# Products of ones at three places of the first block, and one doubling step by upper and lower rows

## The chip, the cores and the metric

The kernel runs on one core of one Trainium2 chip. The metric is device time in microseconds (us), the median over the runs of one launch of the whole program. The engines are TensorE (PE in the profile; its weight loads are PEld), VectorE (DVE), ScalarE (ACT), GpSimd (POOL) and SyncE (SP); here SP issues the DMA transfers.

## What is computed

A two-block network on 256 tokens of width 1024. The first block has two layers: layer 0 mixes tokens with two recurrences side by side (HGRN2 on one half of the width, RWKV7 on the other), layer 1 with attention. The second block has attention, pooling and a mixture of experts. All of the change lies in layer 0's mixer:

```python
def hgrn_rwkv_mixer(h, w_in, w_out, ...):
    u = h @ w_in
    hq, hf, hi, hg, ur = jnp.split(u, ...)
    f = lb + (1.0 - lb) * sigmoid(hf)
    o_a = hgrn2_chunked(silu(hq), 1.0 - f, hi, log(f))
    ...
    y = rwkv7_scan(r, decay, k, v, kk, a)
    o_b = (head_layer_norm(y) + bonus) * g
    return concatenate([o_a, o_b]) @ w_out

def rwkv7_scan(...):
    def step(state, inp):
        sa = einsum('bhvk,bhk->bhv', state, -kk_t)
        state = state * w_t + sa[..., None] * (kk_t * a_t) + v_t[..., None] * k_t
        return state, einsum('bhvk,bhk->bhv', state, r_t)
```

## The kernel before

**Projections.** Weights arrive in fp32 by DMA and are split into a high and a low part (`split_tile`, L112: a cast on ACT at L116, a subtraction on DVE at L117). A product in fp32 accuracy is then three products, high by high, low by high and high by low (`mm3`, L137 to L139). A group of 24 products of 256 columns makes 128 output columns; `dense_tok` makes the values `hv` with 48 products of 512 columns.

**RWKV7 by blocks.** The 256 tokens are two blocks of 128 (b = 0, 1), with 8 heads each, 16 in all. `El` (L556) holds the 128 by 128 lower triangles of all 16. The recurrence is solved by inverting unit lower triangles: the four diagonal blocks of 32 of each triangle go through DRAM (`dd`) into a layout in which DVE eliminates one column after another (`inverse`, L650 and L652: 31 steps of two operations). The result goes back through DRAM (L655, eight reads at L660), and four copies (`Ql`, L661) and four transposes (`Tu`, L664) put it on the diagonals.

**Doublings.** `levels` then joins blocks of 32 into blocks of 64 and those into 128. `first` multiplies `El` by `Tu` (L684), ACT copies the result to `Wm`, and `then` multiplies by `Ql` (L698 for 32, L708 for 64). At l = 32 each of the 8 triangles of a block has one product on its upper 64 rows and one on its lower 64 rows, taken in turn. After that `chain` (from L735) carries the state over the two blocks.

**HGRN2.** Beside this, the projections of `hE` (L800), of the queries `hq` (L816; four groups of 24 products) and of `hv` run, and then nine levels of a score matrix `ST`: DVE prepares `z` (L842, L843, L858, L859), TensorE multiplies it by itself (L865), DVE copies under a mask (L866; L833 for the diagonal).

**Order.** `fills` holds generators whose steps `tick` interleaves with the projections: `pairs` (the other triangles of RWKV7, L607 to L642) and `inverse` in turn, then `levels`, then `chain`. Within that, a scheduler sets each engine's final order; an engine issues in that order. Accumulators in PSUM come from pools: `psa` gives `acc` tiles from one pool of four, in the order of the program's text; `psb` gives `pb` tiles, `psf` gives `pf` tiles. A tile is given again once all uses of it four tiles earlier are done.

**Products of ones.** `spin(n)` (L361) takes one `acc` tile and puts n products of a constant `ones` into it that nobody reads. It stands at three places at the very start of the program.

Of the kernel before, what the change touches and what calls it, by code (L numbers as in the profile page):

```python
# [52 lines left out]
def tile_body(ctx, tc, a, out, stop=None, dbg=None):  # L53
    nc = tc.nc
    V, A, G, T = nc.vector, nc.scalar, nc.gpsimd, nc.tensor
# [12 lines left out]
    def psa():  # L68
        return pa.tile([128, 512], F32, name="acc")
# [17 lines left out]
    ones = const.tile([128, 1], F32, name="ones")  # L87
# [247 lines left out]
    def mixer0():  # L335
# [22 lines left out]
        G.iota(prow, pattern=[[0, 1]], base=0, channel_multiplier=1, allow_small_or_imprecise_dtypes=True)  # L358
        V.tensor_scalar(ident, trow, prow, None, op0=ALU.is_equal)

        def spin(n):  # L361
            p = psa()
            for i in range(n):
                T.matmul(p[:, 0:128], ones.to_broadcast([128, 128]), ones.to_broadcast([128, 128]), start=True, stop=True)
        spin(8)

        raw = [psb(), psb(), psb(), psf()]
# [10 lines left out]
        p = psa()  # L378
# [72 lines left out]
        for s, dst in ((0, ld), (1, ta)):  # L451
            for j2 in range(2):
                p = psb()
                for i in range(2):
                    j = 2 * j2 + i
# [8 lines left out]
        for j2 in range(2):  # L464
            sq = t2([128, 2, S], "sq")
            p = psb()
            for i in range(2):
                j = 2 * j2 + i
# [5 lines left out]
            for i in range(2):  # L474
                j = 2 * j2 + i
# [75 lines left out]
        for b in range(2):  # L551
            bs = slice(b * 128, b * 128 + 128)
            ps = psb(), psb()
            for j in range(4):
                for h in range(2):
                    T.matmul(ps[h][:, j * 128:(j + 1) * 128], al[hp[h], j, bs], bt[0][hp[h], j, bs], start=True, stop=True)  # L556
            for h in range(2):
                V.tensor_tensor(El[:, 8 * b:8 * b + 8, :].rearrange("p (j h) c -> p h j c", h=2)[:, h],
                                ps[h].rearrange("p (j c) -> p j c", j=4), m4(maskL, 4), mult)
# [20 lines left out]
        for b in range(2):  # L580
            p = psb()
# [15 lines left out]
        def pairs():  # L597
            for b in range(2):
                bs = slice(b * 128, b * 128 + 128)
                px = psa()  # L600
                ps = psb(), psb()
                for j in range(4):
                    for h in range(2):
                        T.matmul(ps[h][:, j * 128:(j + 1) * 128], bt[0][hp[h], j, bs], rh[hp[h], j, bs], start=True, stop=True)
                heads = lambda t: t.rearrange("p (j h) c -> p h j c", h=2)
                for h in range(2):
                    V.tensor_tensor(heads(Ebr[b])[:, h], ps[h].rearrange("p (j c) -> p j c", j=4), m4(maskR, 4), mult)  # L607
                yield
                for j2 in range(2):
                    ps = psb(), (psf, psb)[j2]()  # L610
                    for i in range(2):
                        for q_, r in enumerate((al, rh)):
                            for h in range(2):
                                T.matmul(ps[h][:, q_ * 256 + i * 128:q_ * 256 + i * 128 + 128], bt[1][hp[h], 2 * j2 + i, bs],
                                         r[hp[h], 2 * j2 + i, bs], start=True, stop=True)
                    eka = RW.tile([128, 2, 2, 128], F32, name="eka")
                    for h in range(2):
                        V.tensor_tensor(eka[:, h], ps[h][:, 0:256].rearrange("p (i c) -> p i c", i=2), m4(maskA, 2), mult)
                    yield
                    for h in range(2):  # L620
                        V.tensor_tensor(heads(Ekr[b])[:, h, 2 * j2:2 * j2 + 2], ps[h][:, 256:512].rearrange("p (i c) -> p i c", i=2),
                                        m4(maskR, 2), mult)
                    for i in range(2):
                        for h in range(2):
                            hs = slice((2 * j2 + i) * 128 + h * 64, (2 * j2 + i) * 128 + h * 64 + 64)
                            T.matmul(px[:, hs], eka[:, h, i, :], vt[:, b, hs], start=True, stop=True)
                    yield
                A.copy(X[b], px)

            for j2 in range(2):  # L630
                p, p2 = psb(), psf()
                for i in range(2):
                    j = 2 * j2 + i
                    T.matmul(p[:, i * 256:(i + 1) * 256], rk64[:, j, :], rx[:, j, :], start=True, stop=True)
                    T.matmul(p2[:, i * 256:(i + 1) * 256], g2w[:, j * 128:(j + 1) * 128], gd, start=True, stop=True)
                js = slice(2 * j2, 2 * j2 + 2)
                V.tensor_tensor(bon[:, js, :], p.rearrange("p (i t) -> p i t", i=2), vx[:, js, :], mult)
                for i in range(2):
                    j = 2 * j2 + i
                    g = p2[:, i * 256:(i + 1) * 256]  # L640
                    A.activation(gt[:, j, :], g, AF.Copy, scale=col("ln_w", j))
                    V.scalar_tensor_tensor(bon[:, j, :], bon[:, j, :], col("ln_b", j), g, op0=add, op1=mult)  # L642
                yield
# [22 lines left out]
        def mixed(a_, b_):  # L666

            live = [a_, b_]
            while live:
# [2 lines left out]
                        live.remove(g)  # L672
                yield

        def levels():


            def first(l, b):
                o = 8 * b
                Wm = t2([128, 8, l], "Wm")  # L680
                p = psb()[:, 0:8 * l]
                for i in range(8):
                    for r in ((0, 64) if l == 32 else (64,)):
                        T.matmul(p[(r if l == 32 else 0):(r + 64 if l == 32 else 64), i * l:i * l + l],  # L684
                                 El[r:r + 64, o + i, (r if l == 32 else 0):(r + 64 if l == 32 else 64)],
                                 Tu[r:r + 64, o + i, (r + 32 if l == 32 else 64):r + 64], start=True, stop=True)
                n = 128 if l == 32 else 64
                A.copy(Wm[0:n], p[0:n].rearrange("p (h c) -> p h c", h=8))
                return l, b, Wm
# [136 lines left out]
        for l in range(9):  # L826
# [33 lines left out]
            if m < 128:  # L860
                for b in range(2):
                    bs = slice(b * 128, b * 128 + 128)
                    p = psa()
                    for h in range(4):
                        T.matmul(p[:, h * 128:(h + 1) * 128], z[:, h, bs], z[:, h, bs], start=True, stop=True)  # L865
                    V.copy_predicated(part(ST[:, b], l - 1, 1), half4(lvl[:, l - 1, :], l - 1, 1, 4),  # L866
                                      part(p.rearrange("p (h c) -> p h c", h=4), l - 1, 1))
                tick()
                if l == 4:
                    tick(100)  # L870
                    fills.append(chain())
                    tick(2)
            else:
                p = psa()
                for h in range(4):
                    T.matmul(p[:, h * 128:(h + 1) * 128], z[:, h, 0:128], z[:, h, 128:256], start=True, stop=True)
                A.copy(STx, p.rearrange("p (h c) -> p h c", h=4))
# [1157 lines left out]
```

## Time and profile before

| what | value |
|---|---|
| median of 3 runs | 1330.45 us (1330.16 to 1331.88) |
| profiled execution | 1331.68 us, of which its span 1329.8 us |
| PE busy | 1164.5 us, 88% |
| DVE busy | 717.6 us, 54% |
| ACT busy | 497.6 us, 37% |
| mean granted TensorE clock | 0.935 of full |

The span is the time between the first and the last instruction of the trace; 1.9 us of the profiled execution lie around it. The chain that ended last is PE for 52%, DMA for 27% and DVE for 11% of the span. From about 890 us on the expert weights stream at 420 GB/s without a gap; before that TensorE is busy for nine tenths or more of nearly every slice, with the granted clock below full in some.

### The profile page before, as it was taken

The page shows a single profiled execution, that of the slowest core. Times are in us where ns is not written, and L with a number is a line of the kernel's source. Part 1 is how long each engine was busy: PE and PEld are TensorE (multiplying, and loading weights), DVE is VectorE, ACT ScalarE, POOL GpSimd, SP SyncE. Part 2 cuts the span into 40 slices and gives each one's busy share as a digit, 9 for nine tenths or more (in the row PEclk, how much of TensorE's full clock was granted, in tenths as well). Part 3 has the DMA queues.
Part 4 walks back from the last instruction along what each step waited for, and adds up shares of the span by engine and source line. Part 5 has one row for each costly group of instructions (what it writes and reads, how often), then busy time and mean ns, then how long its engine had stood idle before and what let it go on. Part 6 is the DMA issues. An engine that isn't in the chain of part 4 may idle for free.

```text
span 1329.8 us, 18843 instructions
## 1 busy us (share of the span) xinstructions
PE 1164.5 (88%) x7392; PEld 849.3 (64%) x7392; DVE 717.6 (54%) x1293; ACT 497.6 (37%) x870; POOL 208.1 (16%) x218
## 2 busy tenths in 40 slices
PE   8899789999999999999999999898877676777765
PEld 7888787988988888898999888662322121212222
DVE  4768866676777887657665689861112010101112
ACT  7626325454444656546444555620000000000002
POOL 4500010222221351122222232300000000000000
PEclk9899799999999999999999999999987896967797
DMA  8342116768785553667775853699999999999996
GB/s 276 116 119 96 17 65 218 263 240 286 281 291 187 176 184 127 220 232 245 259 246 174 335 190 147 233 366 414 420 422 421 421 420 420 422 418 423 419 422 269
DMA packets 129503, 362.35 MB, mean 272 GB/s; under 512 B 13441, under 2 KB 69505, under 8 KB 105857
## 3 DMA queue, kind: packets, MB, share of 16 engines
q1 hardware_dynamic: 126848, 359.78, 71.9%
q10 hardware_dynamic: 2560, 1.31, 0.4%
q8 instruction: 60, 0.98, 0.3%
q14 instruction: 35, 0.28, 0.1%
HBM read 359.49 MB, written 1.57 MB: 272 GB/s over the span
## 4 chain that ended last, share of the span: by engine, by line
PE 52%; DMA 27%; DVE 11%; issue 4%; ACT 3%; POOL 3%; SPq 0%; ACTq 0%; DVEq 0%; POOLq 0%
DMA ew<-in_exp_w_dram 16%; PE acc L138 9%; PE acc L139 9%; PE acc L137 9%; DMA ew<-in_exp_w2b_dram 8%; PE pb L137 3%; PE pb L139 3%; PE pb L138 3%; DMA wm<-in_mod_w_dram 3%; DVE s L117 2%; PE pb L1733 2%; PE pb L1707 1%; PE pf L1707 1%; PE pb L1699 1%; POOL ul L945 1%
## 5 line engine op out<-in xcount | busy, mean ns | idle before, releaser
L117 DVE TENSOR_TENSOR s<-w,s 128x1024 fp32r<-128x1024 f32 x231 | 294.9, 1280 | 104.8 <-ACT s L116 102.7
L116 ACT CAST s<-w 128x1024 fp32r<-128x1024 f32 x240 | 251.0, 1046 | 129.6 <-PE acc L139 105.0
L137 PE MATMUL pb<-xTh,s 128*128 128x256 f32 x512 | 144.6, 282 | 0.6 <-ACT xTh L147 0.6
L138 PE MATMUL pb<-xTh,s 128*128 128x256 f32 x512 | 144.1, 282 | 0.6 <-DVE s L117 0.6
L139 PE MATMUL pb<-xTl,s 128*128 128x256 f32 x512 | 144.3, 282 | 0.0
L945 POOL TENSOR_TENSOR ul<-u,uh 128x256 fp32r<-128x256 f32 x64 | 88.5, 1382 | 249.2 <-ACT uh L944 249.2
L138 PE MATMUL acc<-s,ul 128*128 128x512 f32 x256 | 100.4, 392 | 1.6 <-POOL ul L945 1.6
L137 PE MATMUL acc<-s,uh 128*128 128x512 f32 x256 | 100.1, 391 | 0.0
L139 PE MATMUL acc<-s,uh 128*128 128x512 f32 x256 | 99.8, 390 | 0.0
L137 PEld LDWEIGHTS pb<-xTh,s 128*128 128x128 f32 x512 | 96.2, 188 | 4.7 <-issue 1.7
L139 PEld LDWEIGHTS pb<-xTl,s 128*128 128x128 f32 x512 | 98.2, 192 | 0.5 <-DVE xTl L148 0.4
L138 PEld LDWEIGHTS pb<-xTh,s 128*128 128x128 f32 x512 | 96.2, 188 | 3.0 <-DVE s L117 1.0
L137 PE MATMUL acc<-xTh,s 128*128 128x256 f32 x320 | 94.3, 296 | 3.2 <-ACT xTh L1228 1.5
L138 PE MATMUL acc<-xTh,s 128*128 128x256 f32 x320 | 92.5, 291 | 3.2 <-POOL s L117 1.9
L139 PE MATMUL acc<-xTl,s 128*128 128x256 f32 x320 | 92.1, 291 | 1.7 <-POOL xTl L389 1.3
L1733 PE MATMUL pb<-ew,big 128*32 128x512 f32 (+1 forms) x544 | 76.4, 680 | 19.0 <-DMA ew<-in_exp_w2b_dram 15.4
L1707 PE MATMUL pb<-ew,big 128*32 128x512 f32 x448 | 68.4, 706 | 27.0 <-DMA ew<-in_exp_w_dram 23.0
L1712 DVE SCALAR_TENSOR_TENSOR big<-big,pb 128x512 f32<-128x512 f32 x8 | 5.5, 688 | 160.2 <-ACT big L1711 160.2
L1707 PE MATMUL pf<-ew,big 128*32 128x512 f32 x448 | 67.6, 714 | 26.3 <-DMA ew<-in_exp_w_dram 26.3
L1573 ACT ACTIVATE big<-pb,mc,gs 128x128 f32<-128x128 f32 x28 | 12.8, 457 | 196.2 <-DVE big L1575 196.2
L316 DVE SCALAR_TENSOR_TENSOR macc<-wm,cond,macc 128x512 f32<-128x512 f32 x84 | 66.0, 808 | 21.3 <-DMA wm<-in_mod_w_dram 21.3
L1766 POOL TENSOR_TENSOR frs<-frs,mhalf 128x1 f32<-128x1 f32 x2 | 1.1, 548 | 437.1 <-DVE frs L1764 437.1
(601 smaller groups left out, 2215.9 us busy)
## 6 DMA issues: line engine op xcount, KB each, us to landing
ew<-in_exp_w_dram SPq DMA_DIRECT2D x128, 1024.0 KB, 19.7
w<-in_w_up_dram SPq DMA_DIRECT2D x32, 1024.0 KB, 5.7
w<-in_w_down_dram SPq DMA_DIRECT2D x32, 1024.0 KB, 5.4
ew<-in_exp_w2a_dram SPq DMA_DIRECT2D x32, 1024.0 KB, 19.8
ew<-in_exp_w2b_dram SPq DMA_DIRECT2D x28, 1024.0 KB, 20.0
wm<-in_mod_w_dram SPq DMA_DIRECT2D x24, 1024.0 KB, 7.8
w<-in_w_in_ar_dram SPq DMA_DIRECT2D x14, 1024.0 KB, 5.3
w<-in_w_qkv_dram SPq DMA_DIRECT2D x12, 1024.0 KB, 5.1
```

Of the source, the lines that this page charges most:

```text
L116: A.copy(hi, src)
L117: (eng or V).tensor_tensor(lo, src, hi, sub)
L137: T.matmul(p, lhs[0], rhs[0], start=start, stop=False)
L138: T.matmul(p, lhs[1], rhs[0], start=False, stop=False)
L139: T.matmul(p, lhs[0], rhs[1], start=False, stop=stop)
L316: V.scalar_tensor_tensor(ac, wq, cond[:, k:k + 1], ac, op0=mult, op1=add)
L945: lows[:] = [G.tensor_tensor(ul, u, uh, sub)]
L1573: A.activation(dst, p, AF.Identity, scale=gs[:, kt:kt + 1], bias=sh[:, kt:kt + 1])
L1699: T.matmul(p[:, i * 128:(i + 1) * 128], x[:, tb, (k0 + i) * 128:(k0 + i + 1) * 128], oo[:, tb, :], start=(tb == 0), stop=(tb == 1))
L1707: T.matmul(p[32 * e:32 * e + 32, :], xg[:, k, 32 * e:32 * e + 32], t[:, e, :], start=(k == 0), stop=(k == KT - 1))
L1712: V.scalar_tensor_tensor(th, th, 1.0, hp[0], op0=add, op1=mult)
L1733: T.matmul(p[32 * e:32 * e + 32, :], ht[:, i, 32 * e:32 * e + 32], t[:, e], start=(i == 0), stop=(i == 3))
```

## The change

`spin` now returns its last product, and with a second argument it is ordered behind a given instruction (`tc.issue_after`). It is called at three more places. Ten products stand behind `El`'s products of block 0. Five stand in `pairs`, behind the first group of block 1. Six stand ahead of the first doubling, behind the last product that the nine score levels have issued by then (`zlast`), then come the eight products of the upper rows, then twelve more products of ones ordered behind those, then the eight of the lower rows. For that the loops of `first` change places: rows outside, triangles inside.

```diff
--- before.py
+++ after.py
@@ -358,10 +358,13 @@
         G.iota(prow, pattern=[[0, 1]], base=0, channel_multiplier=1, allow_small_or_imprecise_dtypes=True)
         V.tensor_scalar(ident, trow, prow, None, op0=ALU.is_equal)
 
-        def spin(n):
-            p = psa()
-            for i in range(n):
-                T.matmul(p[:, 0:128], ones.to_broadcast([128, 128]), ones.to_broadcast([128, 128]), start=True, stop=True)
+        def spin(n, after=None):
+
+            with tc.issue_after(after.ins) if after else nullcontext():
+                p = psa()
+                for i in range(n):
+                    e = T.matmul(p[:, 0:128], ones.to_broadcast([128, 128]), ones.to_broadcast([128, 128]), start=True, stop=True)
+            return e
         spin(8)
 
         raw = [psb(), psb(), psb(), psf()]
@@ -553,7 +556,9 @@
             ps = psb(), psb()
             for j in range(4):
                 for h in range(2):
-                    T.matmul(ps[h][:, j * 128:(j + 1) * 128], al[hp[h], j, bs], bt[0][hp[h], j, bs], start=True, stop=True)
+                    e = T.matmul(ps[h][:, j * 128:(j + 1) * 128], al[hp[h], j, bs], bt[0][hp[h], j, bs], start=True, stop=True)
+            if b == 0:
+                spin(10, e)
             for h in range(2):
                 V.tensor_tensor(El[:, 8 * b:8 * b + 8, :].rearrange("p (j h) c -> p h j c", h=2)[:, h],
                                 ps[h].rearrange("p (j c) -> p j c", j=4), m4(maskL, 4), mult)
@@ -611,8 +616,10 @@
                     for i in range(2):
                         for q_, r in enumerate((al, rh)):
                             for h in range(2):
-                                T.matmul(ps[h][:, q_ * 256 + i * 128:q_ * 256 + i * 128 + 128], bt[1][hp[h], 2 * j2 + i, bs],
-                                         r[hp[h], 2 * j2 + i, bs], start=True, stop=True)
+                                e = T.matmul(ps[h][:, q_ * 256 + i * 128:q_ * 256 + i * 128 + 128], bt[1][hp[h], 2 * j2 + i, bs],
+                                             r[hp[h], 2 * j2 + i, bs], start=True, stop=True)
+                    if b == 1 and j2 == 0:
+                        spin(5, e)
                     eka = RW.tile([128, 2, 2, 128], F32, name="eka")
                     for h in range(2):
                         V.tensor_tensor(eka[:, h], ps[h][:, 0:256].rearrange("p (i c) -> p i c", i=2), m4(maskA, 2), mult)
@@ -672,6 +679,8 @@
                         live.remove(g)
                 yield
 
+        zlast = [None]
+
         def levels():
 
 
@@ -679,11 +688,15 @@
                 o = 8 * b
                 Wm = t2([128, 8, l], "Wm")
                 p = psb()[:, 0:8 * l]
-                for i in range(8):
-                    for r in ((0, 64) if l == 32 else (64,)):
-                        T.matmul(p[(r if l == 32 else 0):(r + 64 if l == 32 else 64), i * l:i * l + l],
-                                 El[r:r + 64, o + i, (r if l == 32 else 0):(r + 64 if l == 32 else 64)],
-                                 Tu[r:r + 64, o + i, (r + 32 if l == 32 else 64):r + 64], start=True, stop=True)
+                for r in ((0, 64) if l == 32 else (64,)):
+                    e = spin(6, zlast[0]) if l == 32 and b == 0 and r == 0 else None
+                    with tc.issue_after(e.ins) if e else nullcontext():
+                        for i in range(8):
+                            e = T.matmul(p[(r if l == 32 else 0):(r + 64 if l == 32 else 64), i * l:i * l + l],
+                                         El[r:r + 64, o + i, (r if l == 32 else 0):(r + 64 if l == 32 else 64)],
+                                         Tu[r:r + 64, o + i, (r + 32 if l == 32 else 64):r + 64], start=True, stop=True)
+                    if l == 32 and b == 0 and r == 0:
+                        spin(12, e)
                 n = 128 if l == 32 else 64
                 A.copy(Wm[0:n], p[0:n].rearrange("p (h c) -> p h c", h=8))
                 return l, b, Wm
@@ -862,7 +875,7 @@
                     bs = slice(b * 128, b * 128 + 128)
                     p = psa()
                     for h in range(4):
-                        T.matmul(p[:, h * 128:(h + 1) * 128], z[:, h, bs], z[:, h, bs], start=True, stop=True)
+                        zlast[0] = T.matmul(p[:, h * 128:(h + 1) * 128], z[:, h, bs], z[:, h, bs], start=True, stop=True)
                     V.copy_predicated(part(ST[:, b], l - 1, 1), half4(lvl[:, l - 1, :], l - 1, 1, 4),
                                       part(p.rearrange("p (h c) -> p h c", h=4), l - 1, 1))
                 tick()
```

The lines of the new file lie 3 to 13 further down: L556 becomes L559, L684 becomes L695, L698 becomes L711, L708 becomes L721, L735 becomes L748, L832 becomes L845, L865 becomes L878, L364 becomes L366. The generator `levels` gives its first step while the query projections are being written down, so that `zlast` holds nothing yet when it is read: the six products are tied to nothing.

**Order on TensorE at the first doubling.** Before, the last products of `hv` (L139), the diagonal scores (L832) and four score levels (L865) stand ahead of the first product that reads `Tu` (L684):

```order
L139 MATMUL acc<-s,xTh 128x512
L832 MATMUL acc<-hq,hE 128x128 x8
L865 MATMUL acc<-zz 128x128 x8
L865 MATMUL acc<-z_1527 128x128 x8
L865 MATMUL acc<-z_1528 128x128 x7
L635 MATMUL pf<-gd,g2w 128x256 x2
L865 MATMUL acc<-z_1528 128x128
L865 MATMUL acc<-zz 128x128 x8
L684 MATMUL pb<-Tu,El 64x32 x32
L698 MATMUL pb<-Ql,Wm 32x32 x16
```

In the changed kernel this is what stands there; the row ahead of it is the last product of the first of the four query groups (L139, `xTl`), and L642 is the old L635:

```order
L139 MATMUL acc<-xTl,s 128x256
L366 MATMUL acc<-ones 128x128 x6
L642 MATMUL pf<-gd,g2w 128x256 x2
L695 MATMUL pb<-Tu,El 64x32 x8
L366 MATMUL acc<-ones 128x128 x12
L695 MATMUL pb<-Tu,El 64x32 x8
L137 MATMUL acc<-xTh,s 128x256
L138 MATMUL acc<-xTh,s 128x256
L139 MATMUL acc<-xTl,s 128x256
```

The products that read `Tu` (now L695) have moved ahead of three query groups (72 products), all 48 products of `hv`, the diagonal scores and the four levels. Behind the piece shown come in turn: one query group; 16 of L695 and 16 of L711; a query group; 8 of L695 and 16 of L711; the last query group; 8 of L695 and 8 of L721; 6 products of `hv`; 8 of L721; the other 42 of `hv`; 8 of L845; 32 of L878 (four levels); L748.

**Order on VectorE at the end of the inverse.** Before, the steps of the inverse (L650, L652) stand among the queries (L816) and the splits of weights (L117):

```order
L816 SCALAR_TENSOR_TENSOR hq<-th,acc 128x256
L652 TENSOR_TENSOR qb<-qb,inv 128x12x10
L816 SCALAR_TENSOR_TENSOR hq<-th,acc 128x256
L650 TENSOR_TENSOR inv<-db,qb 128x121
L117 TENSOR_TENSOR s<-w,s 128x1024
L652 TENSOR_TENSOR qb<-qb,inv 128x11x11
L117 TENSOR_TENSOR s<-w,s 128x1024
L650 TENSOR_TENSOR inv<-db,qb 128x110
L816 SCALAR_TENSOR_TENSOR hq<-th,acc 128x256
L652 TENSOR_TENSOR qb<-qb,inv 128x10x11
L117 TENSOR_TENSOR s<-w,s 128x1024
L650 TENSOR_TENSOR inv<-db,qb 128x108
```

In the changed kernel three of the four queries (now L829) and four of the splits stand behind the copies (L668) and transposes (L671) that follow the inverse:

```order
L668 COPY Ql<-qs 32x2x16x16
L671 STREAM_TRANSPOSE Tu<-Ql 32x16x32
L649 SCALAR_TENSOR_TENSOR bon<-bon,cols,pf 128x256
L668 COPY Ql<-qs 32x2x16x16
L671 STREAM_TRANSPOSE Tu<-Ql 32x16x32
L649 SCALAR_TENSOR_TENSOR bon<-bon,cols,pf 128x256
L668 COPY Ql<-qs 32x2x16x16
L671 STREAM_TRANSPOSE Tu<-Ql 32x16x32
L668 COPY Ql<-qs 32x2x16x16
L671 STREAM_TRANSPOSE Tu<-Ql 32x16x32
L829 SCALAR_TENSOR_TENSOR hq<-th,acc 128x256
L715 STREAM_TRANSPOSE Tu<-pb 32x8x32 x2
```

Behind the inverse have moved, in all, three queries, four splits, the two diagonal mask copies and a net of six operations on `z` and `zz` of 512 columns. On SP the write and reads of the bounce now stand ahead of the last loads of `w_in_ar` and the first of `w_out_ar`.

**Order on TensorE at the first place.** The ten products stand in front of 8 of the 22 products of L559:

```order
L137 MATMUL acc<-xTh,s 128x256
L138 MATMUL acc<-xTh,s 128x256
L139 MATMUL acc<-xTl,s 128x256
L559 MATMUL pb<-bt_620,al 128x128 x3
L366 MATMUL acc<-ones 128x128 x10
L559 MATMUL pb<-bt_620,al 128x128 x8
L588 MATMUL pb<-ident,vx 128x128 x4
```

Before, the 11 products of L556 there stand in one row. At the second place the five products stand among the products of L619 and L633 (the old L614 and L626) of block 1. Behind the doublings, 24 products of L878 stand between L748 and the second block's output, where 11 did, and 12 of L899 and L900 where 8 of L886 and L887 did, and 4 of L889 where 8 of L876 did.

## Rows read from the trace of the kernel before

**Rows 1.** The profile page: the span, and its 40 slices of 33.2 us.

```profile
span 1329.8 us, 18843 instructions
...
PEclk9899799999999999999999999999987896967797
DMA  8342116768785553667775853699999999999996
```

**Rows 2.** Windows: us; busy (x count) of PE, PEld, DVE, ACT, POOL; granted clock; DMA share; GB/s.

```profile
96.00:102.50 6.50, 6.50 (x30) 6.27 (x30) 2.59 (x10) 0.24 (x1) 0.00 (x0) 0.50 0.37 141
147.50:160.00 12.50, 11.97 (x160) 11.44 (x161) 8.18 (x16) 4.79 (x9) 0.00 (x0) 0.50 0.01 3
```

**Rows 3.** Timeline of PE: start us, duration us, line, operation, names, shape, count.

```profile
9.73 1.50 PE L364 MATMUL acc<-ones 128*128 128x128 f32 x12
...
69.12 2.44 PE L556 MATMUL pb<-bt,al 64*128 64x128 f32 x22
```

**Rows 4.** Timeline of DVE, 102 to 141 us; in brackets the idle time before and its releaser.

```profile
102.26 0.42 DVE L800 TENSOR_SCALAR hE<-acc 128x256 f32<-128x256 f32 x1 [3.46 <-PE acc L139]
...
109.04 1.22 DVE L805 TENSOR_TENSOR n<-hE,n 128x1024 f32<-128x1024 f32 x1 [0.99 <-ACT hE L804]
...
125.41 0.69 DVE L842 TENSOR_TENSOR zz<-bc 128x512 f32<-128x512 f32 x1
126.02 0.23 DVE L652 TENSOR_TENSOR qb<-qb,inv 128x78 f32<-128x78 f32 x1
126.17 0.69 DVE L843 TENSOR_TENSOR zz<-bc 128x512 f32<-128x512 f32 x1
...
133.86 0.17 DVE L652 TENSOR_TENSOR qb<-qb,inv 128x16 f32<-128x16 f32 x1
...
140.95 0.41 DVE L661 COPY Ql<-qs 32x512 f32<-32x512 f32 x1
```

**Rows 5.** Groups of DVE by line, 102.2 to 134 us: count | busy us, mean ns | idle.

```profile
L117 DVE TENSOR_TENSOR s<-w,s 128x1024 fp32r<-128x1024 f32 x6 | 7.3, 1218 | 0.1
...
L816 DVE SCALAR_TENSOR_TENSOR hq<-th,acc 128x256 f32<-128x256 f32 x4 | 1.7, 413 | 0.1
L833 DVE COPY_PREDICATED ST<-lvl,acc 128x512 f32<-128x512 uint8 x2 | 1.4, 730 | 0.0
```

**Rows 6.** Timeline of SP's DMA issues at the end of the inverse.

```profile
134.09 0.34 SPq L655 DMA_DIRECT2D dd<-qb  x1
136.08 4.05 SPq L660 DMA_DIRECT2D qs<-dd  x8
```

**Rows 7.** Timeline of PE, 94 to 166 us.

```profile
94.34 0.43 PE L626 MATMUL acc<-vt,eka 128*128 128x64 f32 x2 [1.27 <-DVE eka L618]
...
111.82 0.28 PE L139 MATMUL acc<-xTl,s 128*128 128x256 f32 x1
...
113.86 0.28 PE L139 MATMUL acc<-xTl,s 128*128 128x256 f32 x1
...
120.30 0.39 PE L139 MATMUL acc<-s,xTh 128*128 128x512 f32 x1
...
129.91 0.39 PE L139 MATMUL acc<-s,xTh 128*128 128x512 f32 x1
130.14 1.05 PE L832 MATMUL acc<-hq,hE 128*128 128x128 f32 x8
148.03 3.62 PE L684 MATMUL pb<-Tu,El 64*64 64x32 f32 x60 [3.33 <-DVE Tu L664]
151.58 1.06 PE L698 MATMUL pb<-Ql,Wm 32*32 32x32 f32 x32
...
154.57 1.97 PE L684 MATMUL pb<-Tu,El 64*64 64x64 f32 x16
...
163.19 1.14 PE L708 MATMUL pb<-Wm,Ql 64*64 64x64 f32 x16
164.27 2.00 PE L735 MATMUL pb<-X,Tu 128*128 128x64 f32 x16
```

## The prediction

> **What bounds the kernel now.** I read the page first. By the forty slices the granted clock of TensorE is below full in scattered slices up to about 890 us and the DMA engines are full from there on [rows 1]. The whole change lies in slices 2 to 5, so I then read that stretch: windows for the clock, the timelines of TensorE and VectorE for who waits for whom, the groups of lines for prices, SP's timeline for the bounce through DRAM.
>
> The windows show, behind the second place and at the third, two stretches in which TensorE is busy but granted 0.50, that is 1.2 of 2.4 GHz [rows 2]. Those are what products of ones can win back. The second thing to see is what ends the mixer's middle. VectorE waits 3.46 us for the third group of `hE` and 0.99 us for ScalarE [rows 4]; apart from that it works without a gap, the steps of the inverse one after another with other work between, until the last step at 133.86. The bounce follows: write at 134.09, reads at 136.08 [rows 6], first `Ql` copy at 140.95 [rows 4]. TensorE meanwhile does the queries, `hv` and four score levels, and then stands 3.33 us before the products that read `Tu` run at 148.03; at 164.27 the chain of the state begins [rows 7]. So between 148.03 and 164.27 it has 16.2 us of work ahead of the chain. What stands there in the changed kernel is the question on which this prediction turns.
>
> **The change part by part.** A product of ones in fp32 leaves two records. Twelve records came before the full clock's rate of 0.223 us a product at 9.73 [rows 3]: 1.50 us with the tail of the last, 6 × 0.223 = 1.34 without it. At half clock one is 0.446.
>
> *Place 1.* Ten products, 2.2 us, in front of 8 of `El`'s products. `El`'s 22 records of 69.12 stand without a wait [rows 3], so little hides them. By the third `hE` group, 30 us on, waits in between have taken up part: I take 1.2 us left, bounds 0 and 2.2.
>
> *Place 2.* Five products, 1.1 us, lie in the wait of 1.27 us for `eka` at 94.34 [rows 7] and cost nothing while that wait lasts; without it, 1.1. If they hold the clock, the 24 products of the third `hE` group, the work of the window at 96 [rows 2], fall from 5.4 to 2.7 us. Together with place 1 the read of `hE` comes 2.7 - 1.2 = 1.5 us earlier; bounds: 2.7 earlier, 2.2 later.
>
> *VectorE up to `Tu`.* By the order, four splits (4 × 1.218 = 4.9), three queries (1.2) and two mask copies (1.5) [rows 5] and six operations of 0.69 us [rows 4] now stand behind the inverse. That is 11.7; since each operation overlaps the next by 0.08 us (126.02 + 0.23 against 126.17 [rows 4]), fifteen of them free 10.5. The last dozen steps of the inverse then follow each other directly and lose about 0.1 us each, 1.2. The wait of 0.99 for ScalarE also goes. The inverse ends at 133.9 - 1.5 - 1.0 - 10.5 + 1.2 = 122.1. The bounce takes at least 5.0 us (2.0 from write to reads, 0.5 for the first pair of reads, about 2.5 to land) and at most the 7.1 from 133.86 to 140.95. Two blocks copied and transposed add 2.7. `Tu` can be read first at 129.8 to 131.9; I take 130.5 where it was 144 to 148.
>
> *TensorE behind `Tu`.* This is the largest term. The order puts ahead of the chain, and behind the first product that reads `Tu`: three query groups, `hv`, the diagonal scores, four score levels, the doublings and twelve products of ones. Query products go at (113.86 - 111.82) / 18 = 0.113 us, a group of 24 in 2.72; `hv`'s at (129.91 - 120.30) / 42 = 0.229, 48 in 11.0 [rows 7]. Dense work: 3 × 2.72 + 11.0 = 19.2. Scores: L832's eight records took 1.05 with a tail; eight products, sixteen records, are 16 × 0.112 = 1.79; five such are 8.95. Doublings at half clock: 64 records of L684 at 3.62/60 = 3.9, 2.1 for L698, 2 × 1.97 for the 64s, 2 × 1.14 for L708 [rows 7], 12.2 in all; half that, 6.1, at full clock. Most of them follow dense groups, so I take 8.6. The twelve products of ones come after some 20 us in which TensorE has only two products, so the clock is low: 12 × 0.446 = 5.35. Sum 42.1; all at full clock 36.9; with the doublings and the first query group at half clock 48.4. Against 16.2 before, 26 us of work has lost its cover: it ran beside VectorE's inverse and now waits for its end.
>
> The chain starts at 130.5 + 42.1 = 172.6, and before at 164.27 [rows 7]: +8.3. The six products ahead of `Tu` cost nothing: they lie in the same wait, which is 20 us long. Without it they would cost 6 × 0.446 = 2.7.
>
> *Behind the chain's start.* Nine more products now stand ahead of the second block's output, 9 × 0.223 = 2.0; bounds 0 and 2.0, I take 1.2. The rest of the program follows at its old pace: TensorE stays the limit to about 890 us, and the streams of weights that fill the DMA engines from there on [rows 1] start as buffers come free.
>
> *The doubling by rows.* Upper and lower rows were taken in turn and are now apart. Records of L684 go at 0.06 us each at half clock [rows 7], a quarter of the 0.223 of a full-width record there: 32 columns against 128. That is each product at its own length, with no saving from the neighbour's rows; taking them apart costs nothing, bounds 0 and the 3.9 us above once more. The Trainium skill, TensorEngine Tiling (Array Packing), Key Properties, says that different tiles can execute weight loads and matmuls in parallel; by that rule products in turn would overlap, and taking them apart would add up to 3.9 us. The rows agree with no such overlap here.
>
> **Sum.** 8.3 + 1.2 = +9.5 us. The profiled execution's 1331.68 becomes 1341.2; the median of the runs lies 1.2 below the profiled one, so the runs' median becomes 1340.0.
>
> **The rivals.** *The clock stays low longer.* In the window at 147.5 the clock stayed at 0.50 through 12.5 us of nearly full work [rows 2]. If it does so again behind `Tu`, the first query group (2.7) and part of the doublings add 3 us more: 1343 to 1346. For it: that very row. Against: the dense products from 105 on were granted full speed. Chance 0.15.
>
> *Even.* `Tu` ready at 127.5 (the full 2.7 us at place 2, the bounce at its 5.0) and the list at full clock, 36.9, put the chain at 164.4: no change, 1330 to 1332. Both ends have to come together: 0.12.
>
> *VectorE, not TensorE, ends the mixer: faster.* VectorE is without a gap for 30 us, and the moved work is still its own. If it is so far behind at the chain's start that the chain waits for it or isn't what ends the mixer, TensorE's list costs nothing, and the end comes earlier by the idle time that goes, 3.46 us [rows 4]: 1327.0. It decides if VectorE's backlog when `Tu` is done exceeds the list by more than 8 us, or if the list is under 164.27 - 130.5 = 33.8. Against it: the moved operations are 10.5 us, the list 42. Chance 0.13.
>
> *The order isn't what TensorE waits by.* If query products could pass the waiting product that reads `Tu`, `Tu` would come 13 us earlier at no price and the time would be some 10 us less, 1320. For it nothing; before, TensorE stood 3.33 us at 148.03 [rows 7] with a score level of L865 behind that product in its order. The Trainium skill, TensorE: Matmul & The Clock Gate, Part 2, says that matmuls keep the program's order and only weight loads are taken ahead, which also speaks against it. Chance 0.03.
>
> **How the numbers follow.** My forecast has the remaining 0.57. Slower: 0.57 + 0.15 = 0.72; same: 0.12; faster: 0.13 + 0.03 = 0.16. A measurement of this kernel can tell about 0.2%, 2.7 us, from no change. The range leaves out the faster rivals and the far end of the low clock: from 1329, where the even case ends, to 1346. Within it my own case, with the list between 36.9 and 44 and `Tu` between 129 and 132, gives 1334 to 1343.
>
> **What would show it.** Right: TensorE idle from about 106 to 130 but for a few products; granted clock 0.5 at the first product that reads `Tu`; the inverse's last step near 122; `hv` on TensorE behind the doublings; the chain (L748) near 172. Each step wrong: the third `hE` group still at 0.41 us a product (place 2); the inverse ending after 126 (VectorE); less than 35 us from the first L695 to L748 (the list); a wait of L748 for VectorE (the rival). The prediction falls if the chain starts before 167.

## The result: 1348.8 us, 1.25% slower, and the profile after

| | before | with the change |
|---|---|---|
| median, runs beside each other | 1331.16 (1330.16 to 1335.28, 4 runs) | 1348.77 (1347.33 to 1350.05, 4 runs) |
| ratio, 95% interval | | 1.0125 [1.0106, 1.0144] |
| profiled execution, its span | 1331.68, 1329.8 | 1348.59, 1346.7 |

The direction was forecast, the size wasn't: +17.6 us against +9.5, outside the range. The page's rows that answer to [rows 1]:

```profile
span 1346.7 us, 18973 instructions
...
PEclk9896999999999999999999999999997896978787
DMA  8332114767767544567775864689999999999997
```

The DMA engines are at nine tenths or more from the 28th slice on, where before it was the 27th; a slice is now 33.7 us. Windows of the changed kernel (columns as in [rows 2]) show the shape that was forecast, TensorE nearly idle while VectorE ends the inverse, then full:

```profile
96.00:102.50 6.50, 6.50 (x65) 6.31 (x63) 6.25 (x22) 0.67 (x1) 0.00 (x0) 1.00 0.53 161
105.00:130.00 25.00, 5.94 (x42) 5.31 (x40) 19.88 (x55) 10.00 (x14) 0.96 (x1) 0.65 0.23 59
130.00:177.15 47.15, 44.80 (x419) 41.05 (x418) 29.92 (x48) 16.31 (x25) 0.00 (x0) 0.89 0.23 70
```

VectorE's timeline of the changed kernel answers to [rows 4]: the third `hE` group, the wait for ScalarE, the inverse's last step, the first `Ql` copy, a second wait for ScalarE ahead of the second copy, and the second transpose, the one for which the upper rows wait:

```profile
101.83 0.42 DVE L813 TENSOR_SCALAR hE<-acc 128x256 f32<-128x256 f32 x1
...
108.47 1.22 DVE L818 TENSOR_TENSOR n<-hE,n 128x1024 f32<-128x1024 f32 x1 [1.06 <-ACT hE L817]
...
124.02 0.17 DVE L659 TENSOR_TENSOR qb<-qb,inv 128x16 f32<-128x16 f32 x1
...
129.07 0.42 DVE L668 COPY Ql<-qs 32x512 f32<-32x512 f32 x1 [0.71 <-DMA qs<-dd]
...
131.04 0.48 DVE L649 SCALAR_TENSOR_TENSOR bon<-bon,cols,pf 128x256 f32<-128x256 f32 x1 [0.81 <-ACT gt L648]
...
132.00 0.70 DVE L671 STREAM_TRANSPOSE Tu<-Ql 32x512 f32<-32x512 f32 x1
```

TensorE's timeline of the changed kernel answers to [rows 7]: the six products, the idle stretch, upper rows, the twelve, lower rows, the second block's 16 products, then `hq` by `hE` and the chain:

```profile
107.86 1.50 PE L366 MATMUL acc<-ones 128*128 128x128 f32 x12
128.42 2.08 PE L642 MATMUL pf<-gd,g2w 128*128 128x256 f32 x4 [19.06 <-DVE bon L649]
132.85 1.88 PE L695 MATMUL pb<-Tu,El 64*64 64x32 f32 x16 [2.35 <-DVE Tu L671]
134.66 5.46 PE L366 MATMUL acc<-ones 128*128 128x128 f32 x24
140.05 1.11 PE L695 MATMUL pb<-Tu,El 64*64 64x32 f32 x16
144.03 1.84 PE L695 MATMUL pb<-Tu,El 64*64 64x32 f32 x32
...
168.22 1.95 PE L845 MATMUL acc<-hq,hE 128*128 128x128 f32 x16
...
177.15 1.90 PE L748 MATMUL pb<-X,Tu 128*128 128x64 f32 x16
```

Following the same marks through both traces, the change is 12.9 us behind at the chain's start (177.15 against 164.27), 13.9 at the transposes of the HGRN2 output that close the mixer, 17.6 at the second layer's attention, and 16.9 at the end of the span. So the loss has two parts: the mixer, and in this execution some 4 us in the feed-forward stretch between, where each engine's order is the one of before.

### The profile page after: what moved, and what is told of

It reads as the page before. It is cut to its first block, busy times and chain, and to the rows that moved or that the text cites. A ratio compares the mean times of both kernels' runs of the same rounds, so it can differ in the third digit from the quotient of the medians.

```text
span 1346.7 us, 18973 instructions
## 1 busy us (share of the span) xinstructions
PE 1165.8 (87%) x7458; PEld 851.6 (63%) x7458; DVE 719.1 (53%) x1293; ACT 497.0 (37%) x870; POOL 206.1 (15%) x218
## 4 chain that ended last, share of the span: by engine, by line
PE 50%; DMA 30%; DVE 9%; issue 5%; ACT 3%; POOL 2%; SPq 0%; DVEq 0%; ACTq 0%; POOLq 0%
DMA ew<-in_exp_w_dram 16%; PE acc L138 9%; PE acc L137 9%; PE acc L139 9%; DMA ew<-in_exp_w2b_dram 8%; DMA wm<-in_mod_w_dram 5%; PE pb L137 3%; PE pb L138 3%; PE pb L139 3%; DVE s L117 2%; PE pb L1746 2%; PE pb L1720 1%; PE pf L1720 1%; PE acc L878 1%; PE pb L1712 1%
## 5 line engine op out<-in xcount | busy, mean ns | idle before, releaser
L117 DVE TENSOR_TENSOR s<-w,s 128x1024 fp32r<-128x1024 f32 x231 | 295.8, 1283 | 100.0 <-ACT s L116 99.6
L138 PE MATMUL pb<-xTh,s 128*128 128x256 f32 x512 | 144.3, 282 | 1.8 <-DVE s L117 1.8
L139 PE MATMUL pb<-xTl,s 128*128 128x256 f32 x512 | 144.0, 281 | 0.0
L139 PE MATMUL acc<-s,uh 128*128 128x512 f32 x256 | 99.8, 390 | 0.0
L139 PEld LDWEIGHTS pb<-xTl,s 128*128 128x128 f32 x512 | 98.0, 191 | 0.5 <-DVE xTl L148 0.4
L139 PE MATMUL acc<-xTl,s 128*128 128x256 f32 x320 | 90.8, 287 | 1.4 <-POOL xTl L392 1.3
```

The costliest lines, as they stand in the source:

```text
L117: (eng or V).tensor_tensor(lo, src, hi, sub)
L138: T.matmul(p, lhs[1], rhs[0], start=False, stop=False)
L139: T.matmul(p, lhs[0], rhs[1], start=False, stop=stop)
```

## The experiments

Seventeen runs beside runs of the kernel before. "Tu" is the first product that reads `Tu`, "chain" the start of the chain, "closed" the transposes that close the mixer, "wm" VectorE's whole wait for the transfers of `mod_w` in the feed-forward stretch, all from each run's profile, which is one execution. Kernels whose intervals overlap aren't told apart.

| run | median us | ratio to before [95%] | Tu | chain | closed | wm |
|---|---|---|---|---|---|---|
| before | | | 144.3 | 164.3 | 200.6 | 19.7 |
| the change | 1348.8 | 1.0125 [1.0106, 1.0144] | 132.9 | 177.2 | 214.5 | 32.7 |
| e1 twelve | 1343.3 | 1.0089 [1.0065, 1.0114] | 131.6 | 176.3 | 213.6 | 19.5 |
| e9 twelve again | 1345.5 | 1.0094 [1.0075, 1.0113] | 133.6 | 177.6 | 216.7 | 22.1 |
| e6 place 3 | 1348.4 | 1.0100 [1.0064, 1.0136] | 133.8 | 177.7 | 215.0 | 25.0 |
| e7 twelve, in turn | 1344.6 | 1.0090 [1.0061, 1.0120] | 134.4 | 179.4 | 218.4 | 23.3 |
| e5 the change again | 1349.5 | 1.0125 [1.0094, 1.0156] | 131.9 | 175.5 | 214.5 | 31.1 |
| e12 change, own tile | 1333.6 | 1.0011 [0.9996, 1.0027] | 140.7 | 161.1 | 198.2 | 31.1 |
| e3 places 1 and 2 | 1332.9 | 1.0014 [0.9999, 1.0030] | 141.5 | 161.1 | 200.1 | 24.2 |
| e4 rows apart | 1332.7 | 1.0011 [0.9993, 1.0030] | 142.4 | 162.5 | 202.8 | 19.0 |
| e10 six | 1326.9 | 0.9966 [0.9948, 0.9984] | 139.5 | 158.0 | 195.0 | 23.2 |
| e2 place 3, own tile | 1327.6 | 0.9982 [0.9962, 1.0001] | 139.8 | 157.4 | 194.6 | 24.7 |
| e8 own tile, in turn | 1327.3 | 0.9957 [0.9937, 0.9977] | 141.7 | 157.6 | 195.0 | 24.6 |
| e11 the same and five | 1324.8 | 0.9947 [0.9927, 0.9967] | 138.9 | 152.7 | 191.0 | 24.6 |
| f1 e12 without five | 1331.0 | 0.9996 [0.9979, 1.0014] | 144.6 | 161.2 | 198.1 | 29.6 |
| f2 e12 without ten | 1325.1 | 0.9956 [0.9938, 0.9975] | 137.3 | 153.4 | 192.5 | 29.3 |
| f3 e12 without six | 1338.0 | 1.0037 [1.0014, 1.0059] | 142.4 | 160.9 | 200.8 | 32.5 |
| f4 before and 24 | 1343.1 | 1.0106 [1.0072, 1.0141] | 151.2 | 167.9 | 207.0 | 25.6 |
| f5 e11 and 12 | 1327.8 | 0.9972 [0.9944, 0.9999] | 140.6 | 156.1 | 195.9 | 26.4 |

### Which part carries the loss (e1, e9, e6, e10, e3)

Each leaves products of ones out of the change. e1 and e9 (one kernel) keep the twelve alone, with the rows apart, e6 place 3, e10 the six alone, e3 places 1 and 2 with the doubling of before. The edit of e1 and e9:

```diff
...
-                spin(10, e)
...
-                        spin(5, e)
...
-                    e = spin(6, zlast[0]) if l == 32 and b == 0 and r == 0 else None
+                    e = None
```

> Of the change only the twelve products between upper and lower rows, in a tile of the acc pool; no ten, no five, no six. Theory A (the twelve take an acc tile in program order, so that the three query groups, hv and the score levels behind them have to wait for Tu): nearly all of the loss is here, the chain of the state starts 10 to 15 us later than before, near 175 to 179, and the time is 1343 to 1350. Theory B (the ten and the five at the first two places make TensorE and VectorE late): within 3 us of before, 1328 to 1334.

> Places 1 and 2 alone; the doubling as before. Theory A: next to nothing, minus 2.7 (the third hE group at full clock) to plus 2.2 (ten products late), 1328 to 1334. Theory B (these two places make the loss): over 1340.

> All of place 3 (six, twelve in acc tiles, rows apart), without places 1 and 2. If these two add nothing but chance of the clock: chain start 175 to 178, time 1342 to 1349. If the ten and the five of places 1 and 2 are what makes the change cost 5 us more than the twelve alone, the time is that of the twelve alone, 1341 to 1345.

> The twelve in an acc tile alone, once more, with more runs. The mixer ends 13 us late in it and 14 us late in the whole change, yet the whole change measured 5 us more. If these 5 us belong to the whole change (waits of TensorE for weight splits in the feed-forward stretch: 7.4 and 7.6 us in its two executions, 4.2 to 6.1 in the others), the time stays at 1341 to 1345 and TensorE's waits in that stretch at 4 to 6 us. If they were chance: 1345 to 1350.

> Only the six products ahead of the first doubling, tied to nothing, in an acc tile, rows apart. Theory A: they lie beside other work and order nothing behind Tu; as the run with rows apart alone, 1329 to 1334, chain start 160 to 165. If the six make part of the loss: over 1336.

The twelve alone put the chain 12.0 and 13.3 us late; with the six it is 13.4, with everything 12.9. e9's time lies between its two bands. Places 1 and 2 alone aren't clear of no change. The six alone, in an `acc` tile too, come out faster (0.9966), which I hadn't expected and can't explain. So the twelve carry the mixer's loss. In e10 the queries, `hv` and the levels stand ahead of `Tu` as before; what sets the twelve apart is that they are ordered behind a product that reads `Tu`.

### The same products in another tile (e2, e12)

The six and the twelve now write unused columns of the `pb` tile that the rows' products take anyway; no `acc` tile waits for `Tu`. e2 is place 3 alone, e12 the whole change.

```diff
-        def spin(n, after=None):
+        def spin(n, after=None, into=None):
...
-                p = psa()
+                p = psa()[:, 0:128] if into is None else into
...
-                    e = spin(6, zlast[0]) if l == 32 and b == 0 and r == 0 else None
+                    e = spin(6, zlast[0], pt[:, 256:384]) if l == 32 and b == 0 and r == 0 else None
...
-                        spin(12, e)
+                        spin(12, e, pt[:, 256:384])
```

> Place 3 alone, with six and twelve products written into unused columns of the pb tile that the rows' products write anyway, so that no acc tile is taken; rows apart as in the change. Theory A: the queries, hv and four levels go back ahead of the first product that reads Tu, the loss is gone, and the twelve fill the wait before the rest of Tu: chain start between 158 and 165, time 1324 to 1332. Rival B' (rows apart, or the products of ones between them, cost the time by themselves): chain start after 170, time over 1337.

> The whole change, all three places, rows apart everywhere, with one thing different: the six and the twelve of place 3 go into unused columns of the pb tile instead of acc tiles. Theory A (the acc tile's turn is the loss): the queries, hv and the levels stand ahead of Tu again, chain start 155 to 161, time 1324 to 1331; the difference to the change is 18 to 25 us. If the loss has another part that belongs to places 1 and 2 or to the rows: 1332 to 1340.

TensorE's timeline of e12: the last product of `hv`, the diagonal scores, the first product that reads `Tu`, the twelve, and the chain:

```profile
128.43 0.39 PE L139 MATMUL acc<-s,xTh 128*128 128x512 f32 x1
128.66 1.95 PE L846 MATMUL acc<-hq,hE 128*128 128x128 f32 x16
...
140.72 1.86 PE L696 MATMUL pb<-Tu,El 64*64 64x32 f32 x16 [1.93 <-DVE Tu L671]
142.51 5.38 PE L366 MATMUL pb<-ones 128*128 128x128 f32 x24
...
161.10 1.11 PE L749 MATMUL pb<-X,Tu 128*128 128x64 f32 x9
```

With that alone the queries, `hv` and the levels (three in e12, four in e2) go back ahead of `Tu`, and the whole change falls from 1349 to 1333.6, some 15 us, less than the 18 to 25 expected; place 3 alone comes out level with before (0.9982, interval up to 1.0001). The tile's turn was the loss of the mixer: in e12 it closes at 198.2, before at 200.6. What is left in e12 is the ten of place 1 (below) and the feed-forward stretch, 284.4 us there.

### Rows apart, rows in turn (e4, e7, e8)

e4 has the new loops and no products of ones. e7 has the twelve in an `acc` tile behind block 0's products in turn. e8 is e2 without the six, with block 1 in turn as before.

> Only upper rows and lower rows apart, no product of ones. Theory A: no difference, 1329 to 1333, with the 32 products of 64 by 32 as long as before. Rival (taken in turn they overlapped): plus 2 to plus 4 us, with those 32 products taking 1.5 to 2 times as long.

> The twelve products in an acc tile, but upper and lower rows in turn as before; no ten, five or six. Theory A: queries, hv and levels stay behind Tu, the list from the first product that reads Tu to the chain is only the 2 us shorter that the products of the two row halves gain side by side: 41 to 43 us against 44.3 to 44.6, chain start 172 to 176, time 1339 to 1345. Rival (rows apart is what matters): chain start before 168, time under 1336.

> The twelve products in unused columns of the pb tile, upper and lower rows of block 0 apart with the twelve between, block 1 in turn as before. The clock is held over the wait as in the run with its own tile and half of the products get their overlap back: chain start 155 to 160, time 1323 to 1329, 0.1 to 0.5% under before. If the gain of that run was chance: 1329 to 1333.

TensorE's timelines, first of e4 (rows apart), then of f4, whose order there is that of before (rows in turn), in each the block products that read `Tu`:

```profile
142.38 2.05 PE L691 MATMUL pb<-Tu,El 64*64 64x32 f32 x32 [1.38 <-DVE Tu L667]
146.13 3.62 PE L691 MATMUL pb<-Tu,El 64*64 64x32 f32 x32 [1.70 <-DVE Tu L667]
```

```profile
153.42 2.05 PE L684 MATMUL pb<-Tu,El 64*64 64x32 f32 x60 [1.40 <-DVE Tu L664]
```

32 records apart take as long as 60 in turn: 2.05 us at full clock, 3.62 at half (before, [rows 7]). In turn, the work on upper and lower rows overlaps; apart, a record takes nearly twice as long, half of what one of 128 columns takes and not the quarter that I read from [rows 7] as its own length. Whether two products run at once, or the weight load of one under the product of the other, these rows don't tell. My reading of [rows 7] was wrong here, and the rule of the Trainium skill (TensorEngine Tiling (Array Packing), Key Properties) that different tiles can load and multiply in parallel agrees with these rows. In e4 as a whole it isn't clear of no change. e7's time came out as expected, but its chain missed (179.4 for 172 to 176): after the wait the work takes 42.2 us (137.16 to 179.38), but the first products now need all of `Tu` and stand 2.2 us in between, so that from the first read it is 45.0. e8 keeps rows apart only where the twelve fill that wait, and is clearly below before; so is e10 without the twelve, so the filling isn't shown to be what gains.

### Places 1 and 2 with the loss repaired (e11, f1, f2, f3)

e11 is e8 with the five of place 2. f1, f2 and f3 are e12 without the five, the ten and the six. The edit of e11 against e8:

```diff
...
+                    if b == 1 and j2 == 0:
+                        spin(5, e)
```

> The twelve in the pb tile with block 1 in turn, and the five products of place 2. If place 2 holds the clock where it would have fallen: granted clock 1.00 in the window 96 to 102.5 in every execution, and 1 to 2.7 us less on average than without the five, 1322 to 1327. If the clock's fall there is chance that the five don't move, or they are in the way: 1326 to 1330.

> The run with all places and own tiles, without the five of place 2. In that run and in both executions of the change VectorE waits 31 to 33 us for the transfers of mod_w in the feed-forward stretch, 19 to 25 us in all others. If it is chance of an execution: 19 to 25 here, time 1328 to 1332. If it goes with the ten of place 1 beside place 3: 31 to 33, 1331 to 1335. If it goes with the five: 19 to 25, 1327 to 1331.

> The same without the ten of place 1. If the wait for mod_w goes with the ten: 19 to 25 us and a time of 1325 to 1330, since TensorE isn't late by 2.2 us either; if with the five or the six: 31 to 33 and 1328 to 1333.

> The same without the six of place 3. If the wait for mod_w goes with the six: 19 to 25 us, 1328 to 1332. If it goes with the ten and the five: 31 to 33 us, 1331 to 1336.

e11 has the lowest ratio, 0.53% under before, but its interval overlaps those of e8, e10, f2 and f5, and that of f1, which lacks the five, overlaps e12's: what the five of place 2 are worth isn't shown. e11's windows and TensorE's timeline:

```profile
96.00:102.50 6.50, 6.50 (x48) 6.19 (x47) 6.15 (x19) 3.44 (x4) 0.00 (x0) 1.00 0.26 97
143.00:153.00 10.00, 9.54 (x195) 8.89 (x193) 8.28 (x16) 5.47 (x11) 0.00 (x0) 1.00 0.01 3
```

```profile
138.88 1.11 PE L694 MATMUL pb<-Tu,El 64*64 64x32 f32 x16 [2.15 <-DVE Tu L669]
139.93 2.94 PE L366 MATMUL pb<-ones 128*128 128x128 f32 x24
142.80 2.05 PE L694 MATMUL pb<-Tu,El 64*64 64x32 f32 x48
...
152.72 1.55 PE L747 MATMUL pb<-X,Tu 128*128 128x64 f32 x12
```

The twelve fill the wait, the clock stays at 1.00 through the doublings (before: 0.50 [rows 2]), and from the first read of `Tu` to the chain it takes 13.8 us instead of 20.0. That is the best case: over all executions it is 13.8 to 20.4 with the twelve in their own tile, 16.7 to 20.1 without the twelve, and f4, with the order of before, has the full clock at the first doubling too (the 2.05 us above).

The ten cost more than their 2.2 us: f2 without them is 8.5 us under e12, 5.6 of them by the close of the mixer. VectorE's four reads of `hE` show part of it, first in f2, then in e12:

```profile
76.24 0.42 DVE L812 TENSOR_SCALAR hE<-acc 128x256 f32<-128x256 f32 x1 [3.02 <-PE acc L139]
83.68 0.42 DVE L812 TENSOR_SCALAR hE<-acc 128x256 f32<-128x256 f32 x1 [1.88 <-PE acc L139]
90.99 0.41 DVE L812 TENSOR_SCALAR hE<-acc 128x256 f32<-128x256 f32 x1
99.37 0.42 DVE L812 TENSOR_SCALAR hE<-acc 128x256 f32<-128x256 f32 x1
```

```profile
77.65 0.42 DVE L814 TENSOR_SCALAR hE<-acc 128x256 f32<-128x256 f32 x1 [3.67 <-PE acc L139]
87.03 0.42 DVE L814 TENSOR_SCALAR hE<-acc 128x256 f32<-128x256 f32 x1 [2.53 <-PE acc L139]
93.90 0.42 DVE L814 TENSOR_SCALAR hE<-acc 128x256 f32<-128x256 f32 x1
101.24 0.42 DVE L814 TENSOR_SCALAR hE<-acc 128x256 f32<-128x256 f32 x1
```

With the ten, products of `pairs` have moved ahead of the second group's: in TensorE's timelines 30 records of L619 stand between the first and the second group, where f2 has 20 of its L617. The second group is read 3.4 us later, the last 1.9. `Tu` follows 3.4 us later, and in that execution the twelve ran at half clock (5.38 us for 24 records; 4.57 in f2, 2.94 in e11).

f3 missed both its bands: without the six it is 1338.0, clear above before. With e10 that speaks for the six, but e8, which lacks them and takes block 1 in turn, has a lower ratio than e2, which has them. What they do stays open.

### What is left in the feed-forward stretch (e5, f4, f5)

e5 is the change once more. f4 is the kernel before with `spin(32)` for `spin(8)` at its start; f5 is e11 with `spin(20)` there.

> The changed kernel once more, on the chip of the next three, for the stretch from the transposes of the HGRN2 output to the second layer's attention, which took 280.9 us before, 284.6 with the change and 279.3 to 281.8 in the first four experiments. If the extra 3.7 us belong to this program, the stretch is 283 to 286 again and the time 1346 to 1350; if they are one execution's, it is 279 to 282 and the time 1343 to 1346.

> The kernel before with 24 more products of ones at its first such place (32 for 8), nothing else. VectorE's wait for the mod_w transfers in the feed-forward stretch was 29 to 33 us in all six executions of kernels with 23 or more added products and 19 to 25 us in all eleven with none to 18. If it goes with their number, wherever they stand: 29 to 33 us here. If it goes with their places in the middle of the mixer: 19 to 25 us. The time is 5 to 10 us more than before by the products themselves.

> The fastest kernel so far (five and twelve, 17 added) with 12 more at the first place, 29 in all. If the wait goes with the number: 29 to 33 us where it was 24.6 with 17; if with the places: 22 to 26 us. The time is 1 to 5 us more by the products themselves.

VectorE's waits in that stretch, in the kernel before and in the change again:

```profile
DVE macc L316 <- DMA wm<-in_mod_w_dram: 19.7, 12, 3.4
```

```profile
DVE macc L316 <- DMA wm<-in_mod_w_dram: 31.1, 12, 4.0
```

The stretch took 284.6 us in the change and 282.7 in its second execution, 280.9 before. VectorE waits longer for `mod_w`, the splits of weights stand behind that wait, and TensorE's own waits grow from 5.6 to 7.6 and 7.4 us, in part those for the splits (0.6 to 1.8 and 1.3) and in part those for GpSimd's `ul` (1.2 to 1.8 and 2.4). That the one brings the other is argued, not shown. But the stretch took 282.7 to 284.6 us in the six executions with a wait of 29 us or more and 278.1 to 282.6 in the other thirteen, with 279.3 and 278.1 in e1 and e9. So in these executions the 4 us or so that the whole change costs over the twelve alone lie there. Over the whole program the loads of `mod_w` took longer from issue to landing with the change, 8.2 us in the median against 7.8. The longer wait goes with no single group (f1 to f3 all have 29 us or more, the twelve alone 19.5 and 22.1), nor with the `acc` tile (e12). Over the first seventeen executions it went with the number of added products, 29 us or more from 23 on and 25 or less up to 18; but 24 at the start gave 25.6 (f4) and 29 in all gave 26.4 (f5), between the two (f4's own time rose by 11.5 us, a little over what its products were expected to take). Why these transfers land later stays open.

## Why the prediction was wrong in size

*TensorE's list behind `Tu`: right in kind, and the cause shown.* Idle from 109.4 to 128.4, `hv` behind the doublings, the clock low at the first read, the chain late: all seen. From the first read to the chain it took 44.3 us, forecast 42.1. The failed part is "taking them apart costs nothing": 64 records of L695, at 1.8 + 1.0 + 1.8 us, took 4.6, where the sum's 8.6 for all doublings holds some 2.7 for them (3.9 at half clock, 1.95 at full).

*VectorE up to `Tu`: 2.4 us too early.* "The read of `hE` comes 1.5 us earlier" measured 0.4 (101.83 against 102.26): the third group took 2.9 us where it took 5.3, but began 2.0 us later, where the sum had 1.2 for place 1. "The wait of 0.99 for ScalarE also goes" failed, it is 1.06. That makes the inverse's end 124.02 where 122.1 stood. The bounce took its lower bound (5.05), but from the first copy to the end of the second transpose it took 3.6 us where 2.7 stood, with 0.81 of waiting for ScalarE in front of the second copy: 132.85 for 130.5. The third group's first product, before and with the change:

```profile
96.74 0.58 PE L137 MATMUL acc<-xTh,s 128*128 128x256 f32 x1
```

```profile
98.70 0.38 PE L137 MATMUL acc<-xTh,s 128*128 128x256 f32 x1
```

*Behind the chain's start: right.* 1.2 forecast; 13.9 - 12.9 = 1.0 measured. The agreement is luck in part: by the counts in the section on the change it is 13 products more, 2.9 us, and not nine.

*"The rest of the program follows at its old pace": wrong.* It cost 3.7 us from the mixer's end to the second layer's attention, and 1.9 in the second execution (e5). The order there is unchanged, so I gave it no term and no bound.

So at the second layer's attention, of 17.6 - 9.5 = 8.1 us, 2.4 are `Tu`, 2.2 the list and 3.7 the feed-forward stretch, less 0.2 behind the chain's start; that the medians differ by 17.6 too is chance, the spans differ by 16.9. The mixer's 4.4 us are the larger part and came again in e5, which closes it at 214.5 as well; alone they make 1344.4, inside the range. The range failed because both mixer terms erred the same way and no bound covered the stretch behind them, whose size is that of single executions and whose cause is open.

*Place 2.* The granted clock was 1.00 in its window, as forecast. But it was also 1.00 in e4, where TensorE's order up to the doubling is that of before and the same wait of 1.27 us stands at 93.60. And e1 and e9, one kernel, have:

```profile
96.00:102.50 6.50, 6.50 (x49) 6.11 (x49) 5.28 (x17) 2.49 (x4) 0.00 (x0) 1.00 0.42 155
```

```profile
96.00:102.50 6.50, 6.50 (x33) 6.28 (x34) 2.43 (x9) 0.51 (x1) 0.00 (x0) 0.55 0.30 115
```

One execution's half-clock stretch is no property of the order; I took it for one. With the five all eight executions had 1.00 there; without them four of eleven had 0.50 to 0.55 (before, e6, e7, e9). Whether the five hold the clock stays open.

*The rivals.* That VectorE ends the mixer fell: from 130 on TensorE was busy for 44.80 of 47.15 us, and the chain waited for nothing. That products could pass the waiting one fell: TensorE stood idle up to 128.4 and nothing passed. The clock's staying low fell too: it was 1.00 from 147.5 to 160. "Even" fell with the list at 44.3 and `Tu` at 132.85; its 127.5 for `Tu` doesn't follow from its own terms, which give 128.6.

## What to carry to other kernels

A product that fills a wait must not take its tile from a pool that later, independent work takes in turn: held back behind the wait, it holds that work back too. Put it into spare columns of a tile that the waiting work owns, as e11 does: that takes the loss away; that the products then gain anything isn't shown apart from the rest. And read the changed order of the busiest engine before anything else. An unchanged order far behind the change still deserves a bound of its own; here it moved by 2 to 4 us.

## What the runs showed of the hardware that I had not expected

Products on upper and on lower rows in turn take 0.033 us a record at full clock and 0.059 at half, apart 0.055 and 0.111. The half-clock stretch at 96 us was there before (0.50) and absent in e4 (1.00) with the same order up to it; of two executions of one kernel (e1, e9) one had it. And runs of the kernel before, all told, spread from 1327.4 to 1339.8 us, so that 0.2% needs many runs: the intervals here are 0.15 to 0.4% to either side.
